# Second gate made half by half, sigmoids in two, and a written order for the last prompt pair

## The chip, the cores and the metric

The kernel runs on one core of a Trainium2 chip. The metric is the device time of one execution in microseconds (us). Five engines work side by side, each with its own queue of instructions that it takes in order: TensorE (PE in the profile, its weight loads PEld), the vector engine (DVE), the scalar engine (ACT), GpSimd (POOL) and SyncE (SP). Transfers are issued from the queues of SP, ACT and POOL and carried by 16 DMA engines.

## The reference

One layer of a decoder trunk is computed for two groups with the same weights: a prompt (512 positions) and 8 samples of 8 new positions, each with 4096 earlier positions in a paged cache. In the kernel both lie side by side as 576 columns, of which half 0 is columns 0 to 287 and half 1 the rest. Cut to what matters here:

```python
h = x * (1 + ada[1]) + ada[0]
z = h @ w_in        # q_lat, kv_lat, kr, conv_in, g_a, g_c
o = attention(...)  # prompt: causal softmax in 8 heads; samples: over 32 cached pages each
y_a = o @ w_oa
y_c = (b_g * short_conv(c_g * v_c)) @ w_oc
mix = (sigmoid(g_a) * y_a + sigmoid(g_c) * y_c) @ w_o
x = layer_norm(ALPHA * x + ada[2] * mix)
h2 = x * (1 + ada[4]) + ada[3]
f = (silu(h2 @ w_ff1) * (h2 @ w_ff3)) @ w_ff2
y = layer_norm(ALPHA * x + ada[5] * f)
```

D_MODEL is 1024 (8 blocks of 128 rows, called j below), the feed-forward width 2816 (22 blocks). All matrix products are in float32 by three passes: an operand is split into a high part and the rest, and `mm3` (L118) multiplies low by high (L119), high by low (L120) and high by high (L121).

## The kernel before, in words

Activations are held with the model's dimension on partitions and the 576 columns along the row. Weights come in pieces of 128 x 512 (256 KB); each is split by a copy on ACT (`wh`) and a subtraction on DVE (`wl`), both of line 59 to 64, and then used by TensorE. A piece serves 4 blocks of 128 input rows, so it gives 12 matmuls of 288 columns for one half and 24 for both.

The part around the change has two stages. First the prompt's attention runs in four pairs of heads (`prompt_units`, L478). A pair computes keys, for each of two heads the queries (`qhl`), the scores against the keys (`kt_556` for the even head, `kt_557` for the odd one), a softmax on DVE and ACT over the tile `S` (L500 to L509), then transposes (L518) and products with the values (L526). `merge` mixes filler work into it: the projections of the convolution (`acc<-h`) and the modulation's own product (L202 and L208). What order the scheduler finally gives within that stage is its own choice, by priorities that follow the order of emission.

Second comes the samples' attention, in 36 units (4 pairs of samples, each with its new keys and 8 groups of 4 pages). A unit issues page loads, transposes the previous probabilities (L645, copied by ACT to `pT`), computes scores (L616, L621), takes their maximum and exponential, and multiplies with the values (L658). The whole stage stands in one block with a manual order: every engine does its instructions as they are written. Between the units runs a list of pieces of weights (class `Pieces`): `self.todo` holds them in order, each with a cost, and `take` (L955) does as many after each unit as its share of the costs allows. `go` (L942) does the next item: it loads ahead, splits the next piece and runs its matmuls. What a product needs done with its result waits in `later` (at the next `go`) or in `free` (when `wrote`, L960, is called).

The list: `gated` (the conv gate g_c, its sigmoid, and the product with w_oc), `branches` (the attention gate g_a and the product with w_oa for half 0), `output` (w_o for half 0), `norm` (the first layer norm of half 0: `mean` with one matmul at L829, `center` on DVE and ACT, `variance` with one matmul at L850), `modulated` (rows of `h2`: DVE L884, ACT, DVE L886 for each j) and `feed` (w_ff1 and w_ff3 for half 0 and the first 6 of 22 blocks, with a Silu on ACT). Of gate A, `branches` makes half 0 for all j and half 1 for the first four j; half 1 of the last four stands in `norm`. Half 1's layer norm comes after the samples.

The tile for the input `h` is split by halves: HA and HB. `htile` (L125) gives two buffers in rotation, for HA, HB, then M (the merged branches), h2, ft and a last scratch. Each waits for the readers of the tile two back.

After the block for the samples, the pools close and the rest of the kernel (w_oa for half 1, its norm, the rest of the feed-forward layer, w_ff2) is placed by the scheduler.

Of the kernel before, what the change touches and what calls it, by code (L numbers as in the profile page):

```python
# [7 lines left out]
F32 = mybir.dt.float32  # L8
F32R = mybir.dt.float32r
I32 = mybir.dt.int32  # L10
AF = mybir.ActivationFunctionType
# [9 lines left out]
T = SEQ + NS  # L21
HT = T // 2
# [27 lines left out]
def build(tc, a):  # L50
# [3 lines left out]
    dma = nc.sync.dma_start  # L54
# [3 lines left out]
    def act(out, in_, func=AF.Copy, **kw):  # L58
        nc.scalar.activation(out=out, in_=in_, func=func, **kw)  # L59
# [10 lines left out]
    def pool(name, **kw):  # L70
        p = tc.tile_pool(name=name, bufs=1, reuse_waits="tile", **kw)
        t = p.__enter__()
        pools.append((p, t))
        return t

    def close(t):
        p, u = pools.pop([x[1] for x in pools].index(t))
        p.__exit__(None, None, None)
# [43 lines left out]

    Hp = pool("h")

    def htile(dt=F32R, n=2):  # L125
        return Hp.tile([128, n, 8, HT], dt, tag="h", bufs=2, name="h")

    def gpart(pss, piece, xss, c0, ks, n):

# [43 lines left out]
    keep = pool("keep")  # L173
# [43 lines left out]

    x = XP.tile([128, 8, T], F32, name="x")

    HA, HB = htile(), htile()  # L220
    hs = (halves(HA), halves(HB))

    early = [XP.tile([128, 2, 512], F32, name=f"wa{i}") for i in range(8)]
# [5 lines left out]
    with tc.manual_schedule(engines={mybir.EngineType.SP}):  # L229
        for q in range(4):  # L230
# [39 lines left out]
            for m in range(3):  # L270
                c = slice(256 * m, 256 * m + 256)
# [28 lines left out]
    MT = {"kv": (0, 2), "kr": (2, 1), "q": (3, 3), "conv": (6, 12), "gc": (18, 8), "ga": (26, 8)}  # L300
# [142 lines left out]
    gates = {}  # L443
# [305 lines left out]
    M = []  # L749
# [164 lines left out]
    class Pieces:  # L914
# [27 lines left out]
        def go(self):  # L942
            if not self.todo:
                return
            while self.later:
                self.later.pop(0)()
            src, run, t = self.todo.pop(0)
            self.t += t
            if src is None:
                run()  # L950
            else:
                self.prep()
                run(self.hl.pop(0))
# [26 lines left out]
        def gated(self):  # L980
            gc = gates["gc"]
            for j in range(8):
                yield from self.dense(MT["gc"][0] + j, lambda j=j: gc[:, j],
                                      then=(lambda: act(gc, gc, AF.Sigmoid)) if j == 7 else None)

            def run(w, j):
                pss = [ps_acc(), ps_acc()]
                gemm(pss, [w], [[(ytile[:, 0, k, sl], ytile[:, 1, k, sl]) for k in range(4)] for sl in sls])
                for ps, sl in zip(pss, sls):
                    tt(gc[:, j, sl], gc[:, j, sl], ps[:, :HT], MULT)  # L990
            for j in range(8):
                yield a["w_oc"][j // 2][:, 512 * (j % 2):512 * (j % 2) + 512], lambda w, j=j: run(w, j), 1.0
# [5 lines left out]

        def branches(self):
            def sigmoid():  # L1000
                ga = gates["ga"]
                act(ga[:, :4], ga[:, :4], AF.Sigmoid)
                act(ga[:, 4:, :HT], ga[:, 4:, :HT], AF.Sigmoid)
            for j in range(8):
                yield from self.dense(MT["ga"][0] + j, lambda j=j: self.ga(j), (0, 1) if j < 4 else (0,),
                                      sigmoid if j == 7 else None)

            def run(w, j):
                if not M:
                    M.append(htile())  # L1010
                to_m(j, 0, [w], gates["a3"])

                nc.scalar.dma_start(out=gates["gc"][:, j, :HT], in_=a["xT"][:, j, :HT])
            for j in range(8):
                yield woa(j), lambda w, j=j: run(w, j), 0.5
# [20 lines left out]
        def norm(self):  # L1036

            def sigmoid():
                act(gates["ga"][:, 4:, HT:], gates["ga"][:, 4:, HT:], AF.Sigmoid)

            def variance():
                ga = gates["ga"]
                self.gs, self.bs = (ga[:, 7, 72 * i:72 * i + 72].rearrange("p (j r) -> p j r", r=9) for i in range(2))
                affine(self.gs, self.bs)
                gates["xa"], gates["rst"] = gates["gc"][:, :, :HT], ga[:, 0, :HT]
                self.n.variance(gates["rst"])
            rest = [x for j in range(4, 8) for x in self.dense(MT["ga"][0] + j, lambda j=j: self.ga(j), (1,),
                                                               sigmoid if j == 7 else None)]
            parts = [lambda: self.n.mean(), *(lambda j=j: self.n.center(j, j + 2) for j in range(0, 8, 2)), variance]
            for i, f in enumerate(parts):  # L1050
                yield None, f, 0.1
                yield rest[i]
            yield from rest[len(parts):]

        def modulated(self, j):
            if not j:
                gates["h2"] = htile()

                class Rows:
                    tile = lambda self, shape, dt, tag, bufs, name: (  # L1060
                        gates["a3"].tile(shape, dt, tag=tag, bufs=bufs, name=name))
                self.mod = modulate(Rows(), self.gs, self.bs, gates["rst"], gates["h2"], HT)
            for k in (j, j + 1):
                self.mod(k, None, self.n.d[k])

        def feed(self):

            ps = {}

            def run(w, j, n, p):  # L1070
                if not p:
                    if n:
                        self.wrote()
                    ps[n] = ps_acc()
                gpart([ps[n]], w, [halves(gates["h2"])], 0, range(4 * p, 4 * p + 4), 8)
                if n and p:
                    if not j:
                        gates["ft"] = htile()
                    self.free.append(lambda p1=ps[0], p3=ps[1]: rows(j, p1, p3))

            def rows(j, p1, p3):
                ft = gates["ft"]
                s = gates["a3"].tile([128, HT], F32, tag="mf", bufs=2, name="s")
                act(s, p1[:, :HT], AF.Silu)
                tt(s, s, p3[:, :HT], MULT)
                split(s, ft[:, 0, j], ft[:, 1, j])
            todo = [(a["w_ff3" if n else "w_ff1"][j][:, 512 * p:512 * p + 512],
                     lambda w, j=j, n=n, p=p: run(w, j, n, p), 0.5)
                    for j in range(NF) for n in range(2) for p in range(2)]
            mod = [(None, lambda j=j: self.modulated(j), 0.15) for j in range(0, 8, 2)]  # L1090
            yield from (mod[0], mod[1], todo[0], mod[2], mod[3], *todo[1:])

    def fill_ca():
        ad = fill_ada()
# [7 lines left out]
    def merge(s, f, nf, ns):  # L1102

        done, i = 0, 0
        while i < ns and next(s, None) is not None:
            i += 1
            while done * ns < i * nf:
                u = next(f, None)
                if u is None:
                    break  # L1110
                done += u

    slot = [lambda: None]
    S, F = prompt_units(lambda: slot[0]()), fill_ca()
    merge(S, F, 12, 18)
    for _ in F:
        pass
    close(E2)
    close(E)
    close(CV)  # L1120
# [2 lines left out]
    RP = pool("raw", side="right")  # L1123
    units = [(pa, gg) for pa in range(4) for gg in range(-1, NG)]

    with tc.manual_schedule(engines={getattr(mybir.EngineType, e) for e in ("PE", "Activation", "DVE", "Pool", "SP")}):
        P = Pieces()
# [14 lines left out]
        A3 = gates["a3"] = pool("a3")  # L1142
# [1 line left out]
        while P.todo:  # L1144
            P.go()
        P.wrote()
    close(RP)
    close(A3)
    close(keep)


    XB = pool("xb")
    xr = XB.tile([128, 8, T], F32, name="xr")
    rst1 = XB.tile([128, T], F32, name="rst1")
    l1 = XB.tile([128, 2, 8], F32, name="l1")
    W2 = pool("w2")
    MB = pool("mb")
    LN = pool("ln")
    dma(out=xr[:, :, HT:], in_=a["xT"][:, :, HT:])
    for k in range(0, 8, 2):  # L1160
        act(xr[:, k:k + 2, HT:], xr[:, k:k + 2, HT:], AF.Copy, scale=ALPHA)

# [2 lines left out]
    bs = LN.tile([128, 8, 9], F32, tag="bs", bufs=1, name="bs")  # L1165
    affine(gs, bs)
    h2 = [halves(gates["h2"])]
    M.append(MB.tile([128, 2, 8, HT], F32R, name="mb"))
    for j in range(8):
        P.prep()  # L1170
        to_m(j, 1, [P.hl.pop(0)], LN)
    dma(out=xr[:, :, :HT], in_=gates["xa"])
    dma(out=rst1[:, :HT], in_=gates["rst"])
    close(gates["pool"])
# [15 lines left out]
    n = Norm(LN, xr[:, :, HT:], 1, 6)  # L1190
# [17 lines left out]
    LN = L2  # L1208
# [4 lines left out]
    ft = gates["ft"]  # L1213
# [24 lines left out]
    for js in [range(NF, NF + 3)] + [(j,) for j in (*range(NF), *range(NF + 3, KFF))]:  # L1238
# [6 lines left out]
        if js[0] == NF + 3:  # L1245

            for j in range(8):
                tt(xr[:, j], xr[:, j], rst1, MULT, g)
                g.tensor_scalar(out=xr[:, j], in0=xr[:, j], scalar1=l1[:, 0, j:j + 1], scalar2=l1[:, 1, j:j + 1],
                                op0=MULT, op1=ADD)  # L1250
    lnt = htile(F32)


    names = ["rst", "rs", "rr", "ssum", "qs", "sq0", "sq1", "sg", "mu", "dl"]
    LN = Scratch(names, [lnt[:, k // 8, k % 8] for k in range(len(names))])
    hooks = {}
    for h_ in range(2):
# [13 lines left out]
        n = Norm(LN, xr[:, :, sl], h_, 6)  # L1271
# [153 lines left out]
```

## Time and profile before

| | |
|---|---|
| median of 3 runs | 1153.38 us (1153.24 to 1154.04) |
| profiled execution | 1154.15 us |
| span of its instructions | 1152.4 us |
| mean granted clock of TensorE | 0.967 |
| PE busy | 1062.7 us, 92% |
| DVE busy | 564.5 us, 49% |
| ACT busy | 474.3 us, 41% |
| POOL busy | 205.7 us, 18% |
| bytes by DMA | 203.48 MB, mean 177 GB/s |

The profiled execution's own time is 1.75 us above its span, and 0.77 us above the median. The profile's times are of one execution and count from the first instruction. Busy time is the time in which the engine executes; the granted clock is the share of TensorE's full clock that it was given. In that execution the last product of the prompt's attention (L526) starts at 287.97 us, the first scores of the samples (L621) at 288.68 us and their last transposes (L645) at 666.97 us; the second half's norm and the rest of the feed-forward layer follow to the end.

### The profile page before, as it was taken

How to read it: one execution, taken by the hardware profiler on the slowest of the kernel's cores; microseconds unless marked ns; L12 is line 12 of the kernel's file. 1: busy time of each engine (PE TensorE's matmuls, PEld its weight loads, DVE VectorE, ACT ScalarE, POOL GpSimd, SP SyncE). 2: the span in 40 equal slices, each digit the busy share in tenths (PEclk: the TensorE clock that was granted, in tenths of full speed). 3: DMA queues.
4: the chain of work that ended last, by engine and by line, in shares of the span. 5: the costliest groups of instructions: out<-in, count | busy, mean ns of one | idle time of the engine just before them, and what ended most of it. 6: DMA issues, size and time to landing. Idle time of an engine off the chain costs nothing.

```text
span 1152.4 us, 20041 instructions
## 1 busy us (share of the span) xinstructions
PE 1062.7 (92%) x7646; PEld 924.4 (80%) x7646; DVE 564.5 (49%) x1106; ACT 474.3 (41%) x919; POOL 205.7 (18%) x220
## 2 busy tenths in 40 slices
PE   6889999989999999789779797989999999999994
PEld 5778787868676778657646586989999999999994
DVE  2575354533334433465654456785433333346746
ACT  2564334435344334544553544444322222334433
POOL 1120000020442442244221000171000000001303
PEclk9989999989999999899988998989999999999998
DMA  9626354424787789589766354504422222455551
GB/s 367 214 92 205 138 168 161 163 68 151 261 302 256 256 273 313 183 297 336 258 211 211 118 180 146 165 19 152 141 84 100 75 74 87 126 164 152 164 177 56
DMA packets 92927, 203.48 MB, mean 177 GB/s; under 512 B 12288, under 2 KB 19456, under 8 KB 92832
## 3 DMA queue, kind: packets, MB, share of 16 engines
q1 hardware_dynamic: 72608, 165.36, 42.8%
q10 hardware_dynamic: 16128, 28.45, 7.4%
q0 software_dynamic: 4096, 8.40, 2.2%
q8 instruction: 60, 0.98, 0.4%
q14 instruction: 35, 0.29, 0.1%
HBM read 197.77 MB, written 3.06 MB: 174 GB/s over the span
## 4 chain that ended last, share of the span: by engine, by line
PE 31%; DVE 9%; DMA 7%; ACT 6%; issue 3%; POOL 0%; ACTq 0%; another core or an unknown queue 0%; POOLq 0%; SPq 0%; DVEq 0%
PE acc L119 6%; PE acc L120 6%; PE acc L121 6%; DMA wr<-in_w_ff_dram 5%; PE sc L120 3%; PE sc L121 3%; PE sc L119 3%; DVE wl L62 2%; ACT wh L59 2%; DVE xr L62 2%; PE pv L658 1%; PE sc L621 1%; DMA wr<-in_w_o_dram 1%; DMA raw<-in_page_dram 1%; ACT L59 1%
## 5 line engine op out<-in xcount | busy, mean ns | idle before, releaser
L62 DVE TENSOR_TENSOR wl<-wr,wh 128x512 fp32r<-128x512 f32 (+2 forms) x232 | 208.7, 900 | 256.8 <-ACT wh L59 246.5
L59 ACT ACTIVATE wh<-wr 128x512 fp32r<-128x512 f32 (+2 forms) x234 | 185.2, 793 | 225.8 <-DMA wr<-in_w_ff_dram 74.2
L119 PE MATMUL acc<-h,wl 128*128 128x288 f32 x824 | 254.4, 309 | 18.1 <-ACT h L59 7.3
L120 PE MATMUL acc<-h,wh 128*128 128x288 f32 x824 | 248.2, 301 | 0.4 <-DVE h L886 0.3
L121 PE MATMUL acc<-h,wh 128*128 128x288 f32 x824 | 246.4, 299 | 0.0
L119 PEld LDWEIGHTS acc<-h,wl 128*128 128x128 f32 x824 | 157.2, 191 | 40.0 <-issue 12.9
L556 POOL DMA_INDIRECT kr<-in_krT_dram,idx x128 | 127.0, 992 | 268.1 <-DVE krx L605 140.5
L120 PEld LDWEIGHTS acc<-h,wh 128*128 128x128 f32 x824 | 157.6, 191 | 4.7 <-DVE h L886 2.1
L121 PEld LDWEIGHTS acc<-h,wh 128*128 128x128 f32 x824 | 157.9, 192 | 1.1 <-issue 0.8
L62 POOL TENSOR_TENSOR xr<-xr,h 128x288 f32<-128x288 f32 x16 | 17.2, 1100 | 325.4 <-ACT h L59 321.8
L119 PE MATMUL acc<-f,wl 128*128 128x288 f32 x240 | 71.6, 298 | 1.8 <-DVE wl L62 1.8
L120 PE MATMUL acc<-f,wh 128*128 128x288 f32 x240 | 70.7, 295 | 0.0
L121 PE MATMUL acc<-f,wh 128*128 128x288 f32 x240 | 70.7, 295 | 0.0
L658 PE MATMUL pv<-raw,pT 128*64 128x256 f32 x512 | 62.6, 388 | 3.1 <-ACT pT L59 2.8
L658 PEld LDWEIGHTS pv<-raw,pT 128*64 128x64 f32 x512 | 36.6, 140 | 35.5 <-issue 13.0
L621 PE MATMUL sc<-raw,qa 128*64 128x512 f32 x256 | 63.5, 614 | 0.0
L119 PE MATMUL acc<-hb,wl 128*128 128x288 f32 x168 | 50.1, 299 | 3.9 <-ACT hb L59 3.9
L120 PE MATMUL acc<-hb,wh 128*128 128x288 f32 x168 | 50.6, 301 | 0.2
L121 PE MATMUL acc<-hb,wh 128*128 128x288 f32 x168 | 50.1, 298 | 0.0
L119 PE MATMUL sc<-hb,wl 128*128 128x288 f32 x168 | 49.9, 297 | 0.0
L120 PE MATMUL sc<-hb,wh 128*128 128x288 f32 x168 | 49.9, 297 | 0.0
L121 PE MATMUL sc<-hb,wh 128*128 128x288 f32 x168 | 49.8, 297 | 0.0
(373 smaller groups left out, 2171.6 us busy)
## 6 DMA issues: line engine op xcount, KB each, us to landing
raw<-in_page_dram SPq DMA_DIRECT2D x256, 256.0 KB
wr<-in_w_ff_dram SPq DMA_DIRECT2D x76, 512.0 KB
wa<-in_w_ada_dram SPq DMA_DIRECT2D x40, 512.0 KB
wr<-in_w_in_dram ACTq DMA_DIRECT2D x40, 256.0 KB
wr<-in_w_in_dram SPq DMA_DIRECT2D x32, 256.0 KB
wr<-in_w_ff_dram ACTq DMA_DIRECT2D x24, 256.0 KB
wr<-in_w_ff_dram SPq DMA_DIRECT2D x16, 384.0 KB
wr<-in_w_oa_dram ACTq DMA_DIRECT2D x16, 256.0 KB
```

Of the source, the lines that this page charges most:

```text
L59: nc.scalar.activation(out=out, in_=in_, func=func, **kw)
L62: return (eng or v).tensor_tensor(out=out, in0=in0, in1=in1, op=op)
L119: mm(ps, lhsT=wl, rhs=xh, start=start, stop=False)
L120: mm(ps, lhsT=wh, rhs=xl, start=False, stop=False)
L121: mm(ps, lhsT=wh, rhs=xh, start=False, stop=stop)
L556: g.indirect_dma_start(kr[:, 128 * j:128 * j + 128], None, a["krT"], bass.IndirectOffsetOnAxis(ap=idx[:, i:i + 1], axis=0))
L621: mm(ps[rows(e), :n], lhsT=qa[:, c, 2 * pa + e], rhs=rhs, start=False, stop=c == 1)
L658: mm(pv[rows(e), :KVL], lhsT=pT[:np_, j, e], rhs=rhs, start=j == 0, stop=j == nj - 1)
```

## The change

The second half of gate A is no longer made partly in `branches`. `branches` makes half 0 for all eight j (16 pieces of 12 matmuls, where the first eight pieces had 24), and `norm` makes half 1 for all eight j: 16 pieces of 12. Its parts (mean, four centers, variance, four modulated) are put behind pieces 1, 3, 4, 5, 6, 8, 10, 11, 12 and 13, where the first parts stood before each of the first six pieces, and the modulated rows in `feed`. For HB to stay readable that long, the two buffers of `htile` get a tag each: HA, M, h2 and the last scratch in one, HB and ft in the other. Both sigmoids of gate A are of 8 x 288 columns, and that of the conv gate is done in two halves of four j. `go` calls `wrote` each time, so the Silu rows come at the next piece; `feed` no longer calls it. In the first stage `merge` stops three prompt steps earlier, and the last three are taken in written order on TensorE with two conv steps between. The pools' closing and the eight products with w_oa for half 1 move into the block with the manual order.

```diff
-    def htile(dt=F32R, n=2):
-        return Hp.tile([128, n, 8, HT], dt, tag="h", bufs=2, name="h")
+    def htile(i, dt=F32R):
+        return Hp.tile([128, 2, 8, HT], dt, tag=f"h{i}", bufs=1, name="h")
...
         def go(self):
             if not self.todo:
                 return
-            while self.later:
-                self.later.pop(0)()
+            self.wrote()
             src, run, t = self.todo.pop(0)
...
                 yield from self.dense(MT["gc"][0] + j, lambda j=j: gc[:, j],
-                                      then=(lambda: act(gc, gc, AF.Sigmoid)) if j == 7 else None)
+                                      then=(lambda c=slice(j - 3, j + 1): act(gc[:, c], gc[:, c], AF.Sigmoid))
+                                      if j % 4 == 3 else None)
...
         def branches(self):
             def sigmoid():
-                ga = gates["ga"]
-                act(ga[:, :4], ga[:, :4], AF.Sigmoid)
-                act(ga[:, 4:, :HT], ga[:, 4:, :HT], AF.Sigmoid)
+                act(gates["ga"][:, :, :HT], gates["ga"][:, :, :HT], AF.Sigmoid)
             for j in range(8):
-                yield from self.dense(MT["ga"][0] + j, lambda j=j: self.ga(j), (0, 1) if j < 4 else (0,),
-                                      sigmoid if j == 7 else None)
+                yield from self.dense(MT["ga"][0] + j, lambda j=j: self.ga(j), (0,), sigmoid if j == 7 else None)
...
             def sigmoid():
-                act(gates["ga"][:, 4:, HT:], gates["ga"][:, 4:, HT:], AF.Sigmoid)
+                act(gates["ga"][:, :, HT:], gates["ga"][:, :, HT:], AF.Sigmoid)
...
-            rest = [x for j in range(4, 8) for x in self.dense(MT["ga"][0] + j, lambda j=j: self.ga(j), (1,),
-                                                               sigmoid if j == 7 else None)]
-            parts = [lambda: self.n.mean(), *(lambda j=j: self.n.center(j, j + 2) for j in range(0, 8, 2)), variance]
-            for i, f in enumerate(parts):
-                yield None, f, 0.1
-                yield rest[i]
-            yield from rest[len(parts):]
+            rest = [x for j in range(8) for x in self.dense(MT["ga"][0] + j, lambda j=j: self.ga(j), (1,),
+                                                            sigmoid if j == 7 else None)]
+            parts = [lambda: self.n.mean(), *(lambda j=j: self.n.center(j, j + 2) for j in range(0, 8, 2)), variance,
+                     *(lambda j=j: self.modulated(j) for j in range(0, 8, 2))]
+            places = {1: 0, 3: 1, 4: 2, 5: 3, 6: 4, 8: 5, 10: 6, 11: 7, 12: 8, 13: 9}
+            for i, x in enumerate(rest):
+                yield x
+                if i in places:
+                    yield None, parts[places[i]], 0.1
...
             def run(w, j, n, p):
                 if not p:
-                    if n:
-                        self.wrote()
                     ps[n] = ps_acc()
...
-            mod = [(None, lambda j=j: self.modulated(j), 0.15) for j in range(0, 8, 2)]
-            yield from (mod[0], mod[1], todo[0], mod[2], mod[3], *todo[1:])
+            yield from todo
...
-    merge(S, F, 12, 18)
-    for _ in F:
-        pass
+    merge(S, F, 10, 15)
+    with tc.manual_schedule(engines={mybir.EngineType.PE}):
+        for _ in range(2):
+            next(S)
+            next(F, None)
+        next(S)
+        for _ in F:
+            pass
...
-    close(RP)
-    close(A3)
-    close(keep)
...
+        close(RP)
+        close(A3)
+        close(keep)
...
+        M.append(MB.tile([128, 2, 8, HT], F32R, name="mb"))
+        for j in range(8):
+            P.prep()
+            to_m(j, 1, [P.hl.pop(0)], LN)
...
-    M.append(MB.tile([128, 2, 8, HT], F32R, name="mb"))
-    for j in range(8):
-        P.prep()
-        to_m(j, 1, [P.hl.pop(0)], LN)
```

The next two pieces are TensorE's order in the third pair of prompt heads (4 and 5), where the last scores of head 5 are followed by what comes next: before,

```order
L119 MATMUL sc<-kt_557,qhl 128x512
L120 MATMUL sc<-kt_557,qhl 128x512
L121 MATMUL sc<-kt_557,qhl 128x512
L119 MATMUL acc<-h,wl 128x288
L120 MATMUL acc<-h,wh 128x288
L121 MATMUL acc<-h,wh 128x288
L119 MATMUL acc<-h,wl 128x288
L120 MATMUL acc<-h,wh 128x288
L121 MATMUL acc<-h,wh 128x288
L202 MATMUL acc<-wa,sil 32x256 x4
```

and now:

```order
L202 MATMUL acc<-wa,sil 32x256 x4
L119 MATMUL sc<-kt_557,qhl 128x512
L120 MATMUL sc<-kt_557,qhl 128x512
L121 MATMUL sc<-kt_557,qhl 128x512
L518 MATMUL sc<-ident,S 128x128 x14
L526 MATMUL pv<-pt,vt 64x512 x2
L518 MATMUL sc<-ident,S 128x128 x4
L526 MATMUL pv<-pt,vt 64x384 x2
L518 MATMUL sc<-ident,S 128x128 x2
L526 MATMUL pv<-pt,vt 64x256 x2
```

The conv projections that stood between the scores of head 5 and its transposes have moved behind the scores of the last pair; the transposes (L518) follow the scores at once.

On the vector engine, in the samples' stage, the modulated rows of the first half (`hf` with its buffer number, then `h`): before, the last four of the eight with the splits of weights around them,

```order
L62 TENSOR_TENSOR wl<-wr,wh 128x512
L884 SCALAR_TENSOR_TENSOR hf_6826<-gct,ga 128x288
L886 SCALAR_TENSOR_TENSOR h<-hf_6826,ga,h 128x288
L884 SCALAR_TENSOR_TENSOR hf_6830<-gct,ga 128x288
L886 SCALAR_TENSOR_TENSOR h<-hf_6830,ga,h 128x288
L884 SCALAR_TENSOR_TENSOR hf_6834<-gct,ga 128x288
L886 SCALAR_TENSOR_TENSOR h<-hf_6834,ga,h 128x288
L884 SCALAR_TENSOR_TENSOR hf_6838<-gct,ga 128x288
L886 SCALAR_TENSOR_TENSOR h<-hf_6838,ga,h 128x288
L62 TENSOR_TENSOR wl<-wr,wh 128x512
```

and now the first four:

```order
L62 TENSOR_TENSOR wl<-wr,wh 128x512
L884 SCALAR_TENSOR_TENSOR hf_6593<-gct,ga 128x288
L886 SCALAR_TENSOR_TENSOR h<-hf_6593,ga,h 128x288
L884 SCALAR_TENSOR_TENSOR hf_6597<-gct,ga 128x288
L886 SCALAR_TENSOR_TENSOR h<-hf_6597,ga,h 128x288
L62 TENSOR_TENSOR wl<-wr,wh 128x512
L884 SCALAR_TENSOR_TENSOR hf_6637<-gct,ga 128x288
L886 SCALAR_TENSOR_TENSOR h<-hf_6637,ga,h 128x288
L884 SCALAR_TENSOR_TENSOR hf_6641<-gct,ga 128x288
L886 SCALAR_TENSOR_TENSOR h<-hf_6641,ga,h 128x288
L605 SCALAR_TENSOR_TENSOR krx<-krh,nm,kr 128x512
```

A split of a piece of weights now stands between every two pairs of modulated rows. On TensorE, the mean's matmul of the norm: before,

```order
L121 MATMUL acc<-h,wh 128x288
L829 MATMUL sc<-ga,ones 128x288
L616 MATMUL sc<-krn,qr 128x64 x2
L621 MATMUL sc<-cns,qa 64x64 x4
L658 MATMUL pv<-raw,pT 64x256 x8
```

and now:

```order
L121 MATMUL acc<-h,wh 128x288
L829 MATMUL sc<-ga,ones 128x288
L616 MATMUL sc<-krx,qr 128x512 x2
L621 MATMUL sc<-raw,qa 64x512 x4
L658 MATMUL pv<-raw,pT 64x256 x8
```

The rows read alike, but the `acc<-h` row ahead of L829 was the last product with w_o (its `h` is M) and is now the second piece of gate A's second half (its `h` is HB), 24 matmuls behind the last product with w_o.

More of the change, by code (lines that the diff above doesn't have):

```diff
@@ L218, in build @@
     x = XP.tile([128, 8, T], F32, name="x")
-    HA, HB = htile(), htile()
+    HA, HB = htile(0), htile(1)
     hs = (halves(HA), halves(HB))
@@ L1000, in sigmoid @@
             def sigmoid():
-                ga = gates["ga"]
-                act(ga[:, :4], ga[:, :4], AF.Sigmoid)
-                act(ga[:, 4:, :HT], ga[:, 4:, :HT], AF.Sigmoid)
+                act(gates["ga"][:, :, :HT], gates["ga"][:, :, :HT], AF.Sigmoid)
             for j in range(8):
-                yield from self.dense(MT["ga"][0] + j, lambda j=j: self.ga(j), (0, 1) if j < 4 else (0,),
-                                      sigmoid if j == 7 else None)
+                yield from self.dense(MT["ga"][0] + j, lambda j=j: self.ga(j), (0,), sigmoid if j == 7 else None)
             def run(w, j):
                 if not M:
-                    M.append(htile())
+                    M.append(htile(0))
                 to_m(j, 0, [w], gates["a3"])
@@ L1046, in variance @@
                 self.n.variance(gates["rst"])
-            rest = [x for j in range(4, 8) for x in self.dense(MT["ga"][0] + j, lambda j=j: self.ga(j), (1,),
-                                                               sigmoid if j == 7 else None)]
-            parts = [lambda: self.n.mean(), *(lambda j=j: self.n.center(j, j + 2) for j in range(0, 8, 2)), variance]
-            for i, f in enumerate(parts):
-                yield None, f, 0.1
-                yield rest[i]
-            yield from rest[len(parts):]
+            rest = [x for j in range(8) for x in self.dense(MT["ga"][0] + j, lambda j=j: self.ga(j), (1,),
[7 more added lines that the diff above has]
+                    yield None, parts[places[i]], 0.1
         def modulated(self, j):
             if not j:
-                gates["h2"] = htile()
+                gates["h2"] = htile(0)
                 class Rows:
@@ L1077, in run @@
                     if not j:
-                        gates["ft"] = htile()
+                        gates["ft"] = htile(1)
                     self.free.append(lambda p1=ps[0], p3=ps[1]: rows(j, p1, p3))
@@ L1146, in build @@
         P.wrote()
-    close(RP)
-    close(A3)
-    close(keep)
[L1152 to L1159, printed above, removed]
+        close(RP)
+        close(A3)
+        close(keep)
+        XB = pool("xb")
+        xr = XB.tile([128, 8, T], F32, name="xr")
+        rst1 = XB.tile([128, T], F32, name="rst1")
+        l1 = XB.tile([128, 2, 8], F32, name="l1")
+        W2 = pool("w2")
+        MB = pool("mb")
+        LN = pool("ln")
+        dma(out=xr[:, :, HT:], in_=a["xT"][:, :, HT:])
+        M.append(MB.tile([128, 2, 8, HT], F32R, name="mb"))
+        for j in range(8):
+            P.prep()
+            to_m(j, 1, [P.hl.pop(0)], LN)
     for k in range(0, 8, 2):
@@ L1250, in build @@
                                 op0=MULT, op1=ADD)
-    lnt = htile(F32)
+    lnt = htile(0, F32)
     names = ["rst", "rs", "rr", "ssum", "qs", "sq0", "sq1", "sg", "mu", "dl"]
```

## The prediction

> **What bounds the kernel now.** I read four views in this order: the page's busy times and slices, the busy times by window, TensorE's waits, and the timeline around the longest of them. The page first:
>
> ```profile
> span 1152.4 us, 20041 instructions
> ...
> PE 1062.7 (92%) x7646; PEld 924.4 (80%) x7646; DVE 564.5 (49%) x1106; ACT 474.3 (41%) x919; POOL 205.7 (18%) x220
> ...
> PEclk9989999989999999899988998989999999999998
> ```
>
> TensorE (PE) is busy 92% of the span and nothing else is above half, so the end moves only with TensorE's idle time and with the time in which it runs at a lower granted clock. The third row shows such slices (an 8 where the rest are 9). Both can be found by stage. Columns below: window, length, busy time and count on PE, PEld, DVE, ACT and POOL, granted clock, DMA share, GB/s.
>
> ```profile
> 460.00:520.00 60.00, 50.34 (x312) 35.74 (x309) 32.39 (x72) 28.58 (x56) 21.18 (x21) 0.94 0.74 246
> 520.00:540.00 20.00, 20.00 (x142) 15.35 (x142) 11.24 (x24) 8.77 (x20) 8.52 (x9) 1.00 0.96 339
> 540.00:620.00 80.00, 66.06 (x393) 46.73 (x392) 43.72 (x99) 39.64 (x84) 22.80 (x23) 0.87 0.65 221
> 620.00:680.00 60.00, 52.83 (x346) 41.10 (x344) 26.69 (x55) 30.94 (x57) 0.00 (x0) 0.94 0.47 161
> ...
> 600.00:610.00 10.00, 8.32 (x21) 5.20 (x21) 6.34 (x12) 4.28 (x9) 0.00 (x0) 0.50 0.16 54
> ```
>
> The second row is a stretch without any loss: 142 matmuls in 20 us, 7.1 per us, at clock 1.00. At that rate the others would need 312 / 7.1 = 43.9, 393 / 7.1 = 55.4 and 346 / 7.1 = 48.7 us, so they lose 16.1, 24.6 and 11.3 us. The mix of matmuls differs a little, so these are estimates. The largest loss, 540 to 620, is the first layer norm with the modulation behind it, the place that the change reorders. There 13.9 us are idle (80 less 66.06) and the other 10.7 are slow clock, 0.77 us for each idle one. TensorE's waits (sum, count, longest) there, and then in 460 to 520 and 620 to 720:
>
> ```profile
> PE acc L119 <- ACT h L59: 7.3, 6, 5.2
> PE sc L829 <- DVE ga L62: 3.4, 1, 3.4
> PE sc L850 <- DVE ga L62: 2.6, 1, 2.6
> ...
> PE acc L119 <- DVE wl L62: 3.2, 2, 2.2
> PE sc L645 <- ACT S L59: 2.6, 1, 2.6
> ...
> PE acc L119 <- ACT s L59: 4.8, 3, 2.2
> ```
>
> The first three are the modulation, the mean and the variance: 13.3 of the 13.9 idle us. Their longest, in the timeline (start, length, engine):
>
> ```profile
> 587.83 1.28 ACT L59 ACT_TABLE_LOAD   x1
> 589.12 1.16 ACT L59 ACTIVATE ga<-ga 128x1152 f32<-128x1152 f32 x1
> ...
> 592.29 0.52 DVE L886 SCALAR_TENSOR_TENSOR h<-hf,ga,h 128x288 fp32r<-128x288 f32 x1 [0.60 <-ACT h L59]
> ...
> 598.58 0.61 PE L119 MATMUL acc<-h,wl 128*128 128x288 f32 x1 [5.18 <-ACT h L59]
> ```
>
> The first feed matmul waits 5.18 us for modulated rows, which go DVE, ACT, DVE one by one behind the second sigmoid of the gate, and at 600 to 610 the clock is 0.50.
>
> **The change, part by part.** The sum is made against the profiled execution: 1154.15 us, of which 1152.4 are span. It is 0.77 us above the median of 1153.38.
>
> (1) *The second gate between the norm's parts.* TensorE's work stays the same; 96 matmuls of gate A's second half (8 pieces of weights, 12 matmuls each) come from the stretch before 540 into the norm. Mean, variance and feed then stand two pieces behind what they wait for. A piece of 12 takes 12 / 7.1 = 1.7 us, so two cover 3.4: as long as the mean's 3.4 us wait and longer than the variance's 2.6. The modulation is tighter; vector-engine groups of 556 to 613 (busy, mean ns | idle before and its cause), and one attention unit on TensorE where it runs undisturbed:
>
> ```profile
> L62 DVE TENSOR_TENSOR wl<-wr,wh 128x512 fp32r<-128x512 f32 x10 | 7.1, 706 | 2.9 <-ACT wh L59 1.5 <-issue 1.3
> L886 DVE SCALAR_TENSOR_TENSOR h<-hf,ga,h 128x288 fp32r<-128x288 f32 x8 | 4.1, 518 | 7.4 <-ACT h L59 7.4
> L884 DVE SCALAR_TENSOR_TENSOR hf<-gct,ga 128x288 f32<-128x288 f32 x8 | 4.1, 512 | 0.0
> L605 DVE SCALAR_TENSOR_TENSOR krx<-krh,nm,kr 128x512 fp32r<-128x512 f32 x5 | 3.7, 747 | 1.9 <-ACT krh L59 1.9
> ...
> L629 DVE TENSOR_REDUCE sm<-sc 128x1 f32<-128x512 f32 x3 | 2.0, 683 | 0.0
> ```
> ```profile
> 522.89 0.60 PE L645 MATMUL sc<-ident,S 128*128 128x128 f32 x4
> 524.92 0.63 PE L616 MATMUL sc<-krx,qr 128*128 128x512 f32 x2
> ...
> 527.25 1.90 PE L658 MATMUL pv<-raw,pT 128*64 128x256 f32 x16
> ```
>
> Eight rows take 4.1 + 7.4 + 4.1 = 15.6 us. From the first modulated row to feed TensorE now has five pieces, 8.5 us, and at two pieces a unit two attention units. A unit is 0.6 us of transposes and 4.2 from 524.92 to 529.15: 4.8, two are 9.6. The cover of 18.1 us would do, but the vector engine also splits five weights (3.5) and serves two units (0.747 + 0.683 each, 2.9): 22.0 if none of it fits into the 7.4 us that it waits for ACT. I take that end, 3.9 us uncovered, times 1.77 for the slow clock that goes with it, 6.9, and 1.7 for the small waits that stay: 8.6 of 24.6 are left. That is **-16**. The bounds are -23 (all three waits and their slow clock go, 13.3 x 1.77) and -6 (mean and variance alone, 3.4 + 2.6, the modulation as slow as now).
>
> (2) *Sigmoid of the conv gate in two.* Rows of ACT, and of PE at its end:
>
> ```profile
> 342.32 1.28 ACT L59 ACT_TABLE_LOAD   x1
> 343.62 4.05 ACT L59 ACTIVATE gct<-gct 128x4608 f32<-128x4608 f32 x1
> ...
> 348.72 0.65 PE L658 MATMUL pv<-raw,pT 128*64 128x256 f32 x4 [1.81 <-ACT pT L59]
> ```
>
> ACT is shut for 5.33 us, and the copy that `values` needs is queued behind it: 1.81 us on TensorE. With half of it (about 2.03) done earlier the block is 3.3 us and the wait goes: **-1.8**, between -1.8 and 0 if the earlier half stops another copy for as long.
>
> (3) *First sigmoid of the attention gate*: 2304 columns in place of 3456.
>
> ```profile
> 467.76 3.18 ACT L59 ACTIVATE ga<-ga 128x2304 f32<-128x2304 f32 x2
> ```
>
> By the row above, 2304 columns take some 2.0 us, so 1.2 less in ACT's queue: **-1.2**. The bounds are 0 and the two waits of 460 to 520 together, -5.8.
>
> (4) *Silu rows called earlier* (by `go` before each piece). The row of 4.8 us above is feed waiting for a PSUM buffer that the Silu must free. With it goes its share of the slow clock: of 11.3 lost 7.2 are idle and 4.1 slow, so 4.8 carries 2.7 more. At best -7.5, at worst 0 (the load of a table before each Silu comes anyway). I take **-5**.
>
> (5) *The last prompt pairs in order.* Before, conv and ada matmuls stood between the softmax of the third pair (heads 4 and 5) and its transposes; now they stand in the last pair. What the last pair loses, and how long a softmax takes:
>
> ```profile
> 217.87 0.40 PE L121 MATMUL sc<-kt,qhl 128*128 128x512 f32 x1
> ...
> 222.67 1.27 DVE L509 TENSOR_SCALAR S<-S,sm 128x128 f32<-128x128 f32 x4
> ...
> 244.00 0.47 PE L119 MATMUL sc<-kt,qhl 128*128 128x128 f32 x1 [2.15 <-DVE qhl L62]
> 253.47 0.30 PE L119 MATMUL sc<-kt,qhl 128*128 128x128 f32 x1 [3.19 <-DVE qhl L62]
> ...
> 244.00:260.00 16.00, 12.81 (x67) 12.05 (x68) 7.23 (x28) 5.72 (x20) 3.78 (x4) 0.79 0.38 123
> ```
>
> Removed: the 2.15 us wait, about 1.0 of the 3.19 one (some filler ahead of it), and half of the 2.7 us that 12.81 busy us at 0.79 cost: 4.5. Opened in the third pair: the last score ends at 218.27 and the first of the four scalings is ready near 222.99, 4.7 us in which TensorE now has nothing; a wait for q like the 2.15 one, of which the 16 ada matmuls left there cover little; and 1.4 us of slow clock: 8.2. Net **+3.7**. It would be 0 if the softmax ran much faster without conv work in the vector engine's queue, and +8.2 if the last pair gained nothing.
>
> The Trainium skill, "TensorE: Matmul & The Clock Gate", Part 1, says that the clock halves only after an idle window of about 3.4 us. The trace agrees at 600 to 610 (0.50 behind 5.18 us) and not here, where 0.79 stands beside waits of 2.15 and 3.19. By that page the 1.35 us given back in the last pair would not come and part (5) would be +5.0, the sum 1.3 higher.
>
> (6) *Eight more pieces of weights*, since gate A's first four rows no longer share a piece between halves. Each costs ACT a copy, DVE the 0.706 us row above, and a transfer of 256 KB. ACT's group of 520 to 540:
>
> ```profile
> L59 ACT ACTIVATE wh<-wr 128x512 fp32r<-128x512 f32 x6 | 3.8, 627 | 3.5 <-DMA raw<-in_page_dram 1.3 <-PE acc L121 1.3 <-issue 0.9
> ```
>
> That is 5.0 us of ACT and 5.6 of DVE over 80 us in which they are half busy: hidden by matmuls, as 520 to 540 hides the same pieces of 12 at 0.96 DMA share. I take +1 for pieces that come late; without that cover 2.1 MB at 339 GB/s are 6.2 us. The last attention unit now has no piece between its transposes and its values: +0.8, at most the 1.81 of the row in (2). Together **+1.8**.
>
> (7) *The tail in written order*: the eight products that follow the samples wait for the same splits of weights as before. **0**, 4 either way.
>
> Sum: -16 - 1.8 - 1.2 - 5 + 3.7 + 1.8 + 0 = -18.5, so 1135.7 in the profiled execution's terms and **1134.9 us** for the median.
>
> **Rivals.** (A) *The modulation is the bound*: its rows keep 15.6 us and each stands behind a split of weights on DVE, so matmuls of feed wait as now. For it: the 7.4 us that DVE waits for ACT. Against: the pieces between. Part (1) is -6, the sum -8.5: 1144.9.
>
> (B) *Table loads reach the path.* The instruction order has 27 where there were 23. For it: DVE and ACT feed TensorE in turn here. Against: ACT is busy half the time. Four times the 1.28 us of the row at 342.32 is 5.1, the sum -13.4: 1140.0. The Trainium skill, "ScalarE: Activation LUTs", What ACT_TABLE_LOAD costs, counts a drain of 1.38 us to each load and says to batch by set, against which this change goes; by it four would be 10.6, an estimate that would make the sum -7.9. The trace here shows 1.28 with the next ACTIVATE at once (342.32 to 343.62).
>
> (C) *Weights come late*, slower than before. From the first sigmoid's row on, every piece now has only 12 matmuls, and the queue that just held at 0.96 and 339 GB/s gets 2.1 MB more. If it falls more than the two prefetched pieces behind, the 6.2 us are idle time, 11.0 with slow clock (x 1.77), and since pieces then arrive late the norm is covered by none: 0 for (1). Sum 0 - 1.8 - 1.2 - 5 + 3.7 + 11.0 + 0.8 = +7.5: 1160.9. Against it: 0.65 in 540 to 620, where the pieces go.
>
> (D) *Everything covered*: -23 - 1.8 - 5.8 - 7.5 + 0 + 0.8 = -37.3: 1116.1. It asks for five ends at once.
>
> (E) *The gain is spent elsewhere*: (1) at -6, (4) at 0, (5) at +8.2, rest as taken: -6 - 1.8 - 1.2 + 8.2 + 1.8 = +1.0: 1154.4. The change would then have moved the waits and not removed them.
>
> **How the numbers follow.** My forecast 0.53 (its own range 1128 to 1142); A 0.17, B 0.10, C 0.08, D 0.06, E 0.06. The time is that of the first. The range from 1122 to 1149 takes in A and B and leaves out C, D and E, 0.20 together. A difference of 0.2%, 2.3 us, is what a measurement of this kernel can tell from no change. Forecast, A, B and D are faster: 0.86. E gives 0.05 to the same and 0.01 to slower; with C, slower is 0.09.
>
> **What would show it.** Of the changed kernel: (1) no wait of L829 and L850 over 1 us and the first feed matmul's below 3, clock above 0.9 where it was 0.87; (2) no wait of 1.8 us by L658 behind the conv gate; (4) less than 1 us of `ACT s` waits in feed; (5) a new wait of L518 for `S` of 4 to 5 us near 220 and none of 2.15 near 244; (6) no matmul that waits for `wr` by DMA. I am wrong if the norm's stretch still loses more than 15 us, if (5)'s opening exceeds 9, or if TensorE's waits for `wl` grow by more than 5 us.

## The result and the profile after

The changed kernel takes 1144.56 us (median of 5, 1141.31 to 1145.19) against 1153.38 (1150.46 to 1154.04): ratio 0.9922, 95% interval 0.9903 to 0.9941. It is 8.8 us faster. The prediction was 1134.9, 18.5 us faster; its direction and its range (1122 to 1149) hold, but the gain is only about half of what was said.

The head of the page after (the span; busy time and share; TensorE's clock by slice):

```profile
span 1142.8 us, 20078 instructions
...
PE 1057.4 (93%) x7646; PEld 921.6 (81%) x7646; DVE 570.9 (50%) x1114; ACT 483.3 (42%) x931; POOL 205.5 (18%) x220
...
PEclk9999999899999999899999999989999999999997
```

The same windows as before, of the kernel after (length, busy time and count on PE, PEld, DVE, ACT, POOL, clock, DMA share, GB/s):

```profile
460.00:520.00 60.00, 50.98 (x331) 38.91 (x330) 33.10 (x75) 25.93 (x58) 20.36 (x20) 0.91 0.75 253
520.00:540.00 20.00, 20.00 (x142) 15.35 (x141) 11.43 (x25) 8.37 (x19) 8.58 (x8) 1.00 0.93 319
540.00:620.00 80.00, 70.97 (x458) 50.14 (x456) 46.30 (x105) 45.14 (x93) 24.66 (x24) 0.96 0.77 265
620.00:680.00 60.00, 54.95 (x394) 46.06 (x395) 30.06 (x64) 34.12 (x65) 0.00 (x0) 1.00 0.58 190
...
215.00:245.00 30.00, 25.05 (x148) 18.86 (x149) 10.95 (x26) 7.84 (x18) 6.36 (x9) 0.80 0.23 81
```

In 540 to 620 the clock rose from 0.87 to 0.96 and 458 matmuls are done where there were 393; in 620 to 680 it is 1.00. The last row is new: the third pair of prompt heads, at clock 0.80. TensorE's waits after, in 540 to 620 and in 195 to 290:

```profile
PE acc L119 <- issue: 4.1, 3, 2.5
PE pv L658 <- ACT pT L59: 1.9, 1, 1.9
PE sc L645 <- ACT S L59: 0.9, 1, 0.9
...
PE sc L518 <- DVE S L509: 3.8, 1, 3.8
PE acc L202 <- DMA wa<-in_w_ada_dram: 3.6, 2, 3.3
PE sc L119 <- DVE qhl L62: 3.5, 2, 2.0
PE sc L518 <- ACT pt L59: 0.5, 1, 0.5
```

The three waits of the norm (5.2, 3.4 and 2.6 us by their longest) are gone. The softmax of the third pair (L518 for `S`) and a transfer of the ada weights (`wa`) stop TensorE instead.

Windows of fixed times hold different work in the two kernels. So I compared them by counts: both written orders of TensorE have 6928 matmuls (a float32 one that the profile shows as two is counted once), and the time between the n-th and the m-th is read off each timeline. One execution of each kernel, in us:

| matmuls | what is there | before | after | change, part |
|---|---|---|---|---|
| 300 to 1250 | first pairs | 152.9 | 150.6 | -2.3, no part (an order not changed there) |
| 1250 to 1600 | third and last pair | 61.0 | 69.9 | +8.9, (5) |
| 1600 to 2250 | conv gate | 113.1 | 110.0 | -3.1, (2) |
| 2250 to 3150 | gate A, w_oa, w_o | 171.2 | 173.5 | +2.3, (3) and (6) |
| 3150 to 3400 | norm, modulation | 68.0 | 56.1 | -11.9, (1) |
| 3400 to 3750 | feed | 69.8 | 61.7 | -8.1, (4) |
| 3750 to 4250 | w_oa of half 1, its norm | 87.6 | 90.3 | +2.7, (7) |
| 4250 to 6850 | rest of the feed-forward layer | 348.1 | 349.1 | +1.0 |

The sum is -10.5; behind the 6850th 0.9 come back, and the spans differ by 9.6. The change took some 21 us out of the samples' stage (1600 to 3750: 23 in conv gate, norm and feed, less 2 in gate A) and gave 9 back in the last two prompt pairs.

Equal counts are not everywhere the same matmuls. Part (1) moves 96 of them behind the start of the norm: the mean (L829) is the 3172nd before and the 3064th after, so the rows of gate A and of the norm are safer read together (2250 to 3400: -9.6). One execution also differs from the next by some us, so the runs below say more than this table.

### The profile page after: what moved, and what is told of

Read it like the earlier page. It is cut to its first block, busy times and chain, and to the rows that moved or that the text cites. A ratio compares the mean times of both kernels' runs of the same rounds, so it can differ in the third digit from the quotient of the medians.

```text
span 1142.8 us, 20078 instructions
## 1 busy us (share of the span) xinstructions
PE 1057.4 (93%) x7646; PEld 921.6 (81%) x7646; DVE 570.9 (50%) x1114; ACT 483.3 (42%) x931; POOL 205.5 (18%) x220
## 3 DMA queue, kind: packets, MB, share of 16 engines
HBM read 199.87 MB, written 3.06 MB: 178 GB/s over the span
## 4 chain that ended last, share of the span: by engine, by line
PE 57%; DVE 10%; issue 10%; DMA 9%; ACT 7%; POOL 5%; SPq 1%; ACTq 1%; another core or an unknown queue 0%; POOLq 0%; DVEq 0%
PE acc L119 11%; PE acc L120 10%; PE acc L121 10%; PE sc L119 5%; DMA wr<-in_w_ff_dram 5%; PE sc L120 5%; PE sc L121 5%; POOL kr L556 5%; DVE wl L62 3%; ACT wh L59 3%; PE sc L621 2%; DVE xr L62 2%; PE acc L202 2%; PE pv L658 1%; PE sc L518 1%
## 5 line engine op out<-in xcount | busy, mean ns | idle before, releaser
L62 DVE TENSOR_TENSOR wl<-wr,wh 128x512 fp32r<-128x512 f32 (+2 forms) x240 | 214.3, 894 | 257.8 <-ACT wh L59 227.8
L59 ACT ACTIVATE wh<-wr 128x512 fp32r<-128x512 f32 (+2 forms) x242 | 190.0, 787 | 222.3 <-DMA wr<-in_w_ff_dram 69.7
L658 PE MATMUL pv<-raw,pT 128*64 128x256 f32 x512 | 62.8, 388 | 7.6 <-ACT pT L59 7.6
L658 PEld LDWEIGHTS pv<-raw,pT 128*64 128x64 f32 x512 | 36.5, 139 | 40.0 <-ACT pT L59 12.8
```

The lines of the kernel that those rows point to most:

```text
L62: return (eng or v).tensor_tensor(out=out, in0=in0, in1=in1, op=op)
L658: mm(pv[rows(e), :KVL], lhsT=pT[:np_, j, e], rhs=rhs, start=j == 0, stop=j == nj - 1)
```

## The experiments

The four sets of runs did not all meet a chip of the same speed: the kernel before took 1153.4, 1155.4, 1145.2 and 1154.3 us in them. Times are compared within a set, and otherwise as ratios to the kernel before.

**Part 5 undone.** The whole edit, with all else as in the change:

```diff
-    merge(S, F, 10, 15)
-    with tc.manual_schedule(engines={mybir.EngineType.PE}):
-        for _ in range(2):
-            next(S)
-            next(F, None)
-        next(S)
-        for _ in F:
-            pass
+    merge(S, F, 12, 18)
+    for _ in F:
+        pass
```

> The changed kernel with the two last prompt pairs ordered as before (part 5 undone). By the positions of equal matmul counts in the two traces the two pairs cost 9.0 us more than before (diff of the two kernels -2.3 before them, +6.7 behind them). If that is their price, this kernel is 9 us faster than the changed one: 1135.6 us. Rival: they cost what the prediction said, 3.7, and the rest is an offset of that one execution: 1140.9 us. Second rival: a delay there is absorbed later by waits for transfers: 1144 to 1145 us.

Measured: 1134.73 us against 1155.40, ratio 0.9817 (0.9801 to 0.9833), where the change had 0.9922. The edit is worth 1% of the time. TensorE's waits of this kernel in 195 to 290, and a window:

```profile
PE sc L119 <- DVE qhl L62: 5.3, 2, 3.1
...
215.00:245.00 30.00, 27.85 (x199) 21.55 (x198) 14.34 (x34) 11.25 (x28) 6.34 (x9) 0.96 0.35 110
```

Only the two waits of the last pair are left, and in the third pair 199 matmuls fit where the change fits 148.

**Part 5 alone**, the same lines put into the kernel before:

> The kernel before with the new order of the last two prompt pairs alone (part 5). By the theory that they cost 9.0 us: 1162.4 us, with waits of L518 for S of 3.9 us and of L202 for wa of 3.3 us. By the prediction's 3.7: 1157.1 us. If absorbed later: 1153 to 1154 us.

Measured: 1163.33 us against 1155.40, ratio 1.0080 (1.0058 to 1.0103): 7.9 us slower than before by the medians, 9.2 by the ratio. Its waits in 195 to 290 are those of the change row by row, within 0.1 us, and the interval from 1250 to 1600 takes 69.5 us. So the price is 8 to 9 us without the rest of the change; it is neither 3.7 nor absorbed later.

**The same pair on one chip.** Since the explanation rests on this price, both were run side by side:

> The changed kernel as it is, on the same chip as the three that follow, since the calls before ran on chips on which the kernel before took 1155.4 and 1145.2 us. The ratio to the kernel before should be 0.992 again; if the gain depends on the chip, it differs by more than its interval.

> The changed kernel with the prompt pairs ordered as before, beside the changed one on one chip: 9 to 10 us (0.8 to 0.9%) faster than it, if the price of part 5 is what the first comparison and the two traces say; 3.7 us by the prediction.

Measured: the change 1143.33 (0.9915, 0.9886 to 0.9944), with the old pairs 1134.38 (0.9821, 0.9795 to 0.9847): 9.0 us by the medians, 10.9 by the ratios. The two profiled executions of this set differ by less: their intervals from 1250 to 1600 take 67.6 and 63.2 us. Over all profiled executions that interval takes 59 to 63 us in the seven with the old order of pairs and 67.6 to 71 in the five with the change's, on average 8 apart.

**The ada steps spread.** The change's pair order, but the steps that need `wa` one by one (S is a prompt step, C a conv step, A one ada step):

```diff
+        parts_ca.extend((ad, conv))
...
-        for _ in range(2):
-            next(S)
-            next(F, None)
-        next(S)
+        for step in "SACASACASA":
+            next({"S": S, "C": parts_ca[1], "A": parts_ca[0]}[step], None)
```

> The changed kernel with its own order of prompt pairs, but the ada steps, which stood three in a row behind a conv step, spread one by one between the steps of the last pair. Theory: of part 5's price the 3.3 us wait of L202 for the transfer of wa (and slow clock behind it) comes from three steps in a row on two buffers: spread, it goes, and the kernel is 3 to 5 us faster than the changed one. The softmax wait of 3.9 us in the third pair stays. Rival: the transfer is late in any case, because its buffers come free late: no difference, 0 to 1 us.

Measured: 1137.71 us (0.9855, 0.9824 to 0.9885) beside 1143.33 of the change on that chip: 5.6 us faster, a little more than the 3 to 5 expected. Waits in 195 to 290 and the window of the third pair:

```profile
PE sc L518 <- DVE S L509: 3.9, 1, 3.9
PE sc L119 <- DVE qhl L62: 1.5, 1, 1.5
PE sc L518 <- ACT pt L59: 0.5, 1, 0.5
PE acc L202 <- DMA wa<-in_w_ada_dram: 0.2, 1, 0.2
...
215.00:245.00 30.00, 27.46 (x175) 20.76 (x176) 11.31 (x29) 11.11 (x30) 5.76 (x7) 0.89 0.25 82
```

The softmax wait stays, the transfer's 3.3 us go, the `qhl` wait of 2.0 goes too, and the clock in 215 to 245 is 0.89 where the change on that chip has 0.84. The interval from 1250 to 1600 falls from 67.6 in the change on that chip to 62.0, near the 60.9 and 63.2 of the old order. So over half of part 5's price went with the bunched ada steps (the transfer, one wait for q and slow clock), and not with the lost cover of the softmax. How it divides among these three is not shown, since the spread steps also cover the last pair.

**Filler put by hand into both pairs**, seven filler steps merged before and five at written places of the third and last pair:

```diff
-    merge(S, F, 10, 15)
+    merge(S, F, 7, 10)
...
+        for step in "SFSSFSFSSFSSF":
+            next(S if step == "S" else F, None)
```

> The changed kernel with another written order of the third and last prompt pair: a step of filler stands behind the queries or the scores of each of their heads, so that each softmax and each query has cover. Theory: the price of the change's order is the missing cover in the third pair; with cover in both, the 5.3 us that the last pair waits for qhl before (and their slow clock) go too: 1134.7 - 5 = about 1130 us. Rival: in a written order the filler's own loads of wa stop TensorE (3.3 us at 240 in the changed kernel), once for each step that was moved, and the kernel is no faster than 1134.7, or up to 1140 us.

Measured: 1143.37 us against 1145.18, ratio 0.9984 (0.9965 to 1.0003): no faster than before the change. The rival's cause came true, at a higher price than it gave. Its waits from 150 to 262:

```profile
PE acc L202 <- DMA wa<-in_w_ada_dram: 12.8, 4, 3.3
PE pv L526 <- ACT pt L59: 2.1, 4, 0.7
```

No softmax wait is left, and four of the five filler steps in written order stop 3.1 to 3.3 us for their third load of `wa`: 12.8 us. That is the same wait as the change's one, paid four times. With the filler spread otherwise in the first pairs too, the interval from 300 to 1250 takes some 161 us (152.9 before) and that from 1250 to 1600 some 68.

**Fewer weights.** In gate A's first half the first piece of each two is used twice, which leaves out half of that part of the input projection (`first` keeps the piece `w` that it uses):

```diff
...
+                yield one[0], first, one[2]
+                yield None, lambda keep=keep, two=two: two[1](keep[0]), two[2]
```

> The changed kernel, but in gate A's first half the second of each two pieces of weights is neither loaded nor split: the first one's is used again (that half of the input projection is left out of the result; TensorE's matmuls stay the same in number and place). So it has as many pieces of weights as the kernel before. Theory: the eight added pieces make the queue of weights late, seen in ACT waiting 3.6 us for a w_o piece at 477 and 2.0 us for a w_in piece at 564, which cost TensorE 4.7 and 2.5 us and slow clock behind them: without them the kernel is 8 us faster, 1136.6 us. Rival: the stall at 470 to 490 is the chain of w_oa's pieces on ACT and DVE, and has nothing to do with transfers: 0 to -2 us, 1142.5 to 1144.6 us.

Measured: ratio 0.9885 (0.9870 to 0.9900), 1143.20 us against 1155.40. Against the change's 0.9922 and 0.9915, in other sets, that is 3 to 4 us better; the second interval overlaps. The next kernel, which is the change but for its tail, took 1144.66 in the same set, 1.5 us more. None of this is the 8 of the theory. The waits that it was to remove are these, after:

```profile
480.65 0.63 ACT L59 ACTIVATE wh<-wr 128x512 fp32r<-128x512 f32 x1 [3.56 <-DMA raw<-in_page_dram]
...
483.61 1.12 PE L658 MATMUL pv<-cn,pT 64*64 64x256 f32 x4 [4.67 <-ACT pT L59]
```

With eight pieces fewer, L658 still waits 3.06 us there, and the interval from 2250 to 3150 takes 172.8, as in the change (173.5 and 171.7 in two executions). The late piece at 480 is thus not shown to come from the added pieces. What the eight pieces cost, between 0 and 4 us, stays open.

**The tail outside the manual block**, as before the change:

> The changed kernel with the closing of pools and the eight products of half 1 with w_oa behind the manual block, as before (part 7 undone). By equal matmul counts the changed kernel loses 2.6 us between the first of these products and the second half's feed-forward layer: if the order causes it, 1142.0 us. By the prediction (0): 1144.6 us.

Measured: ratio 0.9909 (0.9894 to 0.9923) beside 0.9922 (0.9903 to 0.9941). No difference can be told, and the interval from 3750 to 4250 stays at 91.8 us. Part 7 costs nothing; why that interval is 1 to 4 us longer than before in the kernels with the change was not found.

**Part 4 undone**, on top of the old pairs:

```diff
-            self.wrote()
+            while self.later:
+                self.later.pop(0)()
...
+                    if n:
+                        self.wrote()
```

> The changed kernel with the prompt pairs as before (that one alone took 1134.7 us, ratio 0.9817) and, on top, the Silu rows called as before (part 4 undone: go empties only the list later, feed calls wrote before a second product). By equal matmul counts feed gained 7.5 us: if the earlier call is the reason, 1142.2 us. By the prediction's 5: 1139.7. Rival: feed gained because the modulated rows no longer stand in it, and the call does nothing: 1134.7.

Measured: 1138.49 us (0.9950, 0.9933 to 0.9966), on the faster chip. Feed (3400 to 3750) takes 70.3 us, as before the change (69.8), where the kernels that share the early call and the new norm take 61.6 to 63.0. The waits for the Silu (`ACT s`) are back, 590 to 700:

```profile
PE acc L119 <- DVE wl L62: 11.2, 8, 3.6
PE acc L119 <- ACT s L59: 5.1, 3, 2.4
```

Feed's whole gain is the earlier call. The kernel with the conv gate's sigmoid in one piece, below, ran in the same set; it has the early call and is 8.1 us faster (1130.35).

**Parts 1, 3 and 6 undone**, on top of the old pairs: `branches`, `norm` and the modulated rows in `feed` as in the diff's lines before.

> The changed kernel with the prompt pairs as before and, on top, gate A's halves, their sigmoids, the norm's places and the modulated rows in feed as before (parts 1, 3 and 6 undone). By equal matmul counts the norm gains 12.9 us and the first gate with w_oa and w_o loses 1.4: together 11.5, so 1146.2 us. By the prediction's terms (16 + 1.2 - 1.8 = 15.4): 1150.1 us. Rival: most of the norm's gain is the waits of feed that the earlier Silu rows take away anyway: under 5, 1139 us or less.

Measured: 1140.56 us (0.9956, 0.9935 to 0.9978), 10.2 us slower than the 1130.35 of the kernel with the sigmoid in one piece in the same set. The norm (3150 to 3400) takes 68.9 us, as before (68.0), against 54.8 to 56.1 in the kernels with the new norm. Its waits in 520 to 620 are those of the kernel before:

```profile
PE acc L119 <- ACT h L59: 7.1, 4, 5.2
PE sc L829 <- DVE ga L62: 4.1, 1, 4.1
PE sc L850 <- DVE ga L62: 2.9, 1, 2.9
```

Feed is at 60.8 in this kernel although the modulated rows stand in it again, so the two gains are separate.

**The conv gate's sigmoid in one piece**, on top of the old pairs:

```diff
-                                      then=(lambda c=slice(j - 3, j + 1): act(gc[:, c], gc[:, c], AF.Sigmoid))
-                                      if j % 4 == 3 else None)
+                                      then=(lambda: act(gc, gc, AF.Sigmoid)) if j == 7 else None)
```

> The changed kernel with the prompt pairs as before and, on top, the conv gate's sigmoid in one piece (part 2 undone). By equal matmul counts the half gained 2.3 us, by the prediction 1.8: 1136.5 to 1137.0 us, with a wait of L658 for pT of 1.8 us behind it. Rival: the wait is taken up by slack later: 1134.7.

> The changed kernel with the prompt pairs as before and the conv gate's sigmoid in one piece, beside the one with the sigmoid in two on one chip: 1.8 us slower by the prediction, 2.3 by the traces. Rival: no difference, since each half loads a table of its own.

Measured: 1130.35 us (0.9865, 0.9847 to 0.9883) on the faster chip, where its counterpart with two did not run; then, beside that counterpart, 1138.11 against 1134.38 (ratios 0.9856, 0.9829 to 0.9882, and 0.9821, 0.9795 to 0.9847). One piece is 3.7 us slower, with intervals that overlap; the interval from 1600 to 2250 takes 113.1 us with one and 110.0 with two. The wait of L658 (start, length, engine) with one piece:

```profile
347.39 1.95 PE L658 MATMUL pv<-raw,pT 128*64 128x256 f32 x16 [1.74 <-ACT pT L59]
```

With two it is not there. On the faster chip the interval is 107.8 with one and 107.5 in the kernels with two, so there the half gained next to nothing. The same holds in the set of the first experiments: part 5 alone, with one piece, takes 111.4 there, and the kernels with two take 111.1 to 111.2.

The best of these is the change with the old pairs, 0.9817 and 0.9821: 20 us faster than before.

## Why the prediction was right and wrong

**The step that failed is (5)**, "the last prompt pairs in order", net +3.7 with bounds 0 and +8.2. It measured 8.9 by the timelines, 7.9 to 9.2 alone and 9.0 to 10.9 on one chip. The idle time that was named came as forecast; one wait was left out, and the slow clock was charged too low. In the timeline of the third and last pair after (start, length, wait):

```profile
209.01 0.33 PE L119 MATMUL sc<-kt,qhl 128*128 128x128 f32 x1 [1.48 <-DVE qhl L62]
216.19 2.61 PE L518 MATMUL sc<-ident,S 128*128 128x128 f32 x11 [3.85 <-DVE S L509]
...
240.44 0.67 PE L202 MATMUL acc<-wa,sil 128*32 128x256 f32 x8 [3.29 <-DMA wa<-in_w_ada_dram]
260.15 0.30 PE L119 MATMUL sc<-kt,qhl 128*128 128x128 f32 x1 [2.03 <-DVE qhl L62]
```

- The softmax wait is 3.85 and 0.5 where 4.7 was said, the wait for q in the third pair 1.48 where it was 2.15, and the last pair's 5.3 fell to 2.0. These are right.
- The transfer of `wa` (3.29 us) was not in the sum. I had counted the moved filler's matmuls and not its loads: a conv step carries three ada steps, each with its own load, and the scheduler had spread them over the gaps. In written order the third waits each time, as the placed kernel shows four times over. The spread kernel gives 5.6 us back.
- The slow clock was charged with 1.4 us for 6.9 us of new waits, though part (1) had taken 0.77 us for each idle one. The window from 215 to 245 has 25.05 busy us at 0.80, so 5.0 us lost, against 27.85 at 0.96, so 1.1, with the old order. With 0.77 per idle us and the transfer, the same working gives (6.9 + 3.3 - 3.2) x 1.77 = 12.4, above the 9 measured; with neither it gave 3.7. Measured, the waits of 195 to 290 grew from 5.3 to 11.4 us, 6.1 more. The stretches at half clock there (last section) cost about 7 us after and 3.4 before, an estimate from half of TensorE's busy time in them. Together that is some 9.7, against 8.9 by the timelines.
- By the sign that the prediction itself named, an opening above 9 us, (5) was wrong: the new waits alone, 1.48, 3.85, 0.5 and 3.6 us, come to 9.4.

**All the rest together came out near its sum**: without (5) that was -22.2, and the change with the old pairs is 20.7 us (1155.40 to 1134.73) and 19.9 us faster than before. In part this is luck: (1) with (3) and (6) gained less than said, (2) and (4) more. Within it:

- (1) *-16*: measured -11.9. Mean and variance wait no more and the feed's first matmul waits 0.78 us. What is left are 4.1 us of `issue`, 1.9 of L658 and slow clock, so the residue was mis-sized, not the mechanism. By the prediction's own estimate 540 to 620 still loses 80 - 458 / 7.1 = 15.5 us, just over the 15 that it named as a sign of being wrong. The longest of these waits stands behind a copy of weights that is itself late, by the profile for a transfer, which the prediction did not have:

```profile
566.45 0.63 ACT L59 ACTIVATE wh<-wr 128x512 fp32r<-128x512 f32 x1 [2.00 <-DMA raw<-in_page_dram]
...
567.86 0.40 PE L119 MATMUL acc<-h,wl 128*128 128x288 f32 x1 [2.53 <-issue]
```

  It stays at 2.16 us with eight pieces fewer, so the added pieces are not its cause.
- (2) *-1.8*: 3.1 by the timelines, 3.7 by the times of one chip, next to nothing on two others. Its wait of 1.8 us is the right one.
- (3) and (6), *-1.2 and +1.8* (0.8 of it in a later row): +2.3 and +0.5 in two executions. Their sign was not settled. The last attention unit's wait is 1.84 us (L658 at 655.20), the upper bound. Together with (1), the rows from 2250 to 3400 take 225 to 230 us in the eleven executions with the new norm and 239 to 242 in the three without: some 12 less, where -16.2 was forecast.
- (4) *-5*: -8.1. The upper bound of 7.5 was nearer; the waits for `ACT s` (4.8 us before, 5.1 with the early call undone) vanish in the change. Those for `wl` in 590 to 700 grew from 6.0 to 9.7, less than the 5 us that would have spoken against the prediction.
- (7) *0*: confirmed within what the runs can tell.

**The rivals.** (A), the modulation as the bound at 1144.9, gave the measured time and not its reason: the norm gained 11.9, not 6. (C), late weights, is not seen as a bound of the change: with the pieces taken away 0 to 4 us came. For (B), table loads on the path, one wait of TensorE after, 0.90 us for `S` at 463.04, stands behind a load of 1.28 us at 460.91; before, 2.57 us stood behind the same one at 476.07. No other wait above 1 us in the samples' stage stands right behind one. The Trainium skill, "ScalarE: Activation LUTs", Table sets: the hidden batching unit, says to batch by set; the sigmoid in two, which goes against it, was not slower here, by time or by timeline.

## What to carry to other kernels

Price a step of work by all that it issues, its loads above all: filler that a scheduler had spread over gaps needs its transfers in the same places, and a written order that bunches more loads than there are buffers makes TensorE wait for a buffer to be emptied and filled again. When idle time lies on TensorE, add the slow clock that follows with one and the same factor in every term. A comparison of two timelines at equal counts of matmuls tells the parts of a change from each other when its whole time cannot, as long as no work has moved over the borders and more than one execution is read.

## What was not expected of the hardware

The slow clock of a window is a mean of stretches at full and at half clock, and the half ones reach beyond the wait. Two windows of the kernel after, then one of the kernel before:

```profile
213.60:223.80 10.20, 7.14 (x26) 4.02 (x26) 1.45 (x5) 4.71 (x14) 0.00 (x0) 0.50 0.06 24
223.90:240.80 16.90, 13.61 (x110) 11.12 (x106) 7.96 (x14) 4.53 (x10) 3.38 (x5) 1.00 0.21 73
...
244.00:247.00 3.00, 3.00 (x11) 2.90 (x12) 1.08 (x5) 0.00 (x0) 2.11 (x3) 0.50 0.14 44
```

After, the waits of 1.48 and 3.85 us end at 209.01 and 216.19, and 7.14 busy us at 0.50 lose 3.6 us more. Before, the clock is 0.50 right behind a wait of 2.15 us. The Trainium skill, "TensorE: Matmul & The Clock Gate", Part 1, in its table of states, ties a halved clock to an idle window of about 3.4 us, which the 3.85 us wait agrees with. The 0.50 behind 2.15 us does not agree, nor does the 0.78 in 245 to 270 of the kernel with the old pairs, beside waits of 2.6 us and less:

```profile
245.00:270.00 25.00, 22.36 (x125) 20.99 (x123) 12.30 (x35) 12.01 (x32) 2.20 (x3) 0.78 0.56 191
...
PE sc L119 <- DVE qhl L62: 4.8, 2, 2.6
```
